# A row-wise softmax over 4096 rows: one tile's load shared between SyncE and GpSimd, and the first tile's load in one piece

## The chip, the cores and the metric

The kernel runs on one core of one Trainium2 chip. The metric is the device time of one execution in microseconds; the median of several runs is compared. Nothing is computed on the host.

## The reference

```python
batch, seq, vocab = 16, 256, 32768          # logits, fp32; temperature = 1.0
scaled = logits / temperature
scaled = scaled - scaled.max(axis=-1, keepdims=True)
exp_scaled = np.exp(scaled)
return (exp_scaled / exp_scaled.sum(axis=-1, keepdims=True)).astype(np.float32)
```

That is 4096 rows of 32768 numbers: 537 MB are read and 537 MB written.

## The kernel before

**Tiles.** Each row is cut into two halves of `_W` = 16384 numbers, and each half lies on one of the 128 partitions. A tile is 64 rows, that is 128 partitions of 64 KB each, 8 MB in all; there are 64 tiles. The buffer `xs` has three slots of 64 KB per partition, so tile g uses slot g mod 3, and it is worked on in place: load, exponentiate, scale, store.

**Work on a tile.** A tile is cut into three pieces of columns (six in the last two tiles). VectorE takes each piece's maximum (line 207); ScalarE exponentiates the piece with that maximum and sums it (line 267). Then VectorE brings the two halves of each row together in a few instructions of less than half a microsecond (lines 225 to 252), and the pieces are multiplied by their factors: the first on ScalarE (line 286), the others on VectorE (line 258). VectorE and ScalarE go through the tiles in order; the first four and the last three are written out, those between run in a loop.

**Transfers.** All DMAs are issued by SyncE (SP) in an order written out by hand: loads 0, 1, 2, store 0, load 3, store 1, store 2, and then load i and store i-1 in turn. A load of tile g waits until the store of tile g-3 has landed, because it overwrites its slot; a store waits until its tile is scaled (the wait stands at lines 150 to 155, the store at line 160, the load at line 143). SP issues in order, so a wait of one holds up all that stand behind it. A transfer is spread over the core's 16 DMA engines; its semaphore has risen by 16 when all of it has landed. Signals of one key add up over the transfers that share it.

**The places that the change touches.** `load_parts` says in which parts a tile is loaded. The first tile (g = 0) has two: 15360 columns of all rows, and the last `_NARROW` = 1024 columns. That second part is issued as 19 transfers (line 141) over the rows that `narrow_rows` gives:

```python
step = p // _FEW                       # 128 // 7 = 18
return [slice(q, step * _FEW, step) for q in range(step)] + [slice(step * _FEW, p)]
```

that is, 18 transfers of seven rows that are 18 apart, and one of the last two rows. The third tile (g = 2) is one transfer of 128 rows. In `landed`, VectorE waits for a part's semaphore before the first piece that touches it. Tile 3 uses the same slot and the same semaphores as tile 0, so its values there count on from tile 0's. GpSimd issues nothing in this kernel apart from four small constants.

Of the kernel before, what the change touches and what calls it, by code (L numbers as in the profile page):

```python
# [8 lines left out]
_W = 16384  # L9
# [1 line left out]
_PLAIN = ((6304, 5376, 4704), (0,))  # L11
_LATE = ((4096, 3072, 3072, 2048, 2048, 2048), (3, 4, 5))
_LAST_STORES = ((0, 4096), (4096, 6144), (10240, 6144))
_NARROW = 1024
_FEW = 7
_HEAD = 4
_TAIL = 3

# [45 lines left out]


def load_parts(g):
    if g == 0:
        return [(0, _W - _NARROW), (_W - _NARROW, _NARROW)]
    if g == 3:
        return [(0, _W // 2), (_W // 2, _W // 2)]  # L70
    return [(0, _W)]


def store_parts(g, n):
    if g == 0:
        return [(0, _W // 2), (_W // 2, _W // 2)]
    return list(_LAST_STORES) if g == n - 1 else [(0, _W)]


def narrow_rows(p):  # L80
    step = p // _FEW
    return [slice(q, step * _FEW, step) for q in range(step)] + [slice(step * _FEW, p)]


def order(n):
# [7 lines left out]
def kernel(  # L93
# [6 lines left out]
    nc = tc.nc  # L100
    inv_t = 1.0 / float(temperature)
    P = nc.NUM_PARTITIONS
    fp32 = mybir.dt.float32
# [7 lines left out]
    x = xf.rearrange("n (h v) -> (n h) v", h=2)  # L111
# [8 lines left out]
    X = nc.alloc_sbuf_tensor("xs", [P, _BUFS * _W], fp32)  # L120
    T = [nc.alloc_sbuf_tensor(f"t{q}", [P, 4 * most], fp32) for q in range(_BUFS)]
    E = [nc.alloc_sbuf_tensor(f"ee{q}", [P, 2 * most], fp32) for q in range(_BUFS)]
    J = [nc.alloc_sbuf_tensor(f"junk{q}", [P, 2 * most], fp32) for q in range(_BUFS)]
    R = [nc.alloc_sbuf_tensor(f"row{q}", [P, 4], fp32) for q in range(_BUFS)]
    sig = Signals(nc)
    stored = {}

    def load(g):
        p = Place(g, G)
        rows = slice(g * P, (g + 1) * P)  # L130
        for j, (s, n) in enumerate(load_parts(g)):
            if g >= _BUFS:
                parts = store_parts(g - _BUFS, G)
                for i, (a, m) in enumerate(parts):
                    if a < s + n and s < a + m:
                        nc.sync.wait_ge(*stored[g - _BUFS][i])
            where = slice(p.slot * _W + s, p.slot * _W + s + n)
            key = ("ld", j, *p.key)
            if g == 0 and j == 1:
                for some in narrow_rows(P):  # L140
                    sig.dma(key, nc.sync.dma_start(out=X[some, where], in_=x[some, s : s + n]))
            else:
                sig.dma(key, nc.sync.dma_start(out=X[:, where], in_=x[rows, s : s + n]))

    def store(g):
        p = Place(g, G)
        rows = slice(g * P, (g + 1) * P)
        stored[g] = []
        for i, (s, n) in enumerate(store_parts(g, G)):
            if p.looped:  # L150
                nc.sync.wait_ge(sig[("scaled", *p.key)], 2 * p.n)
            else:
                for group in (p.own, p.on_act):
                    for k in [k for k in group if k in p.over(s, n)][-1:]:
                        nc.sync.wait_ge(sig[("scaled", k, *p.key)], p.n)
            where = slice(p.slot * _W + s, p.slot * _W + s + n)
            stored[g].append(
                sig.dma(
                    ("st", i, p.slot),
                    nc.sync.dma_start(out=o[rows, s : s + n], in_=X[:, where]),  # L160
                )
            )

    class Work:

        def __init__(self, p):
            self.p = p
            q = p.slot
            K = self.K = len(p.pieces)
            self.t, self.e, self.j, self.r = T[q], E[q], J[q], R[q]  # L170
            self.tv = self.t[:, 0 : 4 * K].rearrange("p (a b k) -> p a b k", a=2, b=2)
# [18 lines left out]
        def landed(self, engine, k, seen):  # L190
            s, n = self.p.pieces[k]
            for j, (a, m) in enumerate(load_parts(self.p.g)):
                if a < s + n and s < a + m and j not in seen:
                    seen.add(j)
                    times = len(narrow_rows(P)) if self.p.g == 0 and j == 1 else 1
                    value = self.p.n16
                    if self.p.g == 3 and j == 1:
                        value, times = 16 * len(narrow_rows(P)) + 16, 1
                    engine.wait_ge(sig[("ld", j, *self.p.key)], value * times)

        def vector(self):
            t, e, r, tv, f, K = self.t, self.e, self.r, self.tv, self.j, self.K
# [85 lines left out]
    for what, g in order(G):  # L288
        if what == "L":
            load(g)  # L290
        else:
            store(g)
    for key in [key for key in sig.made if key[0] == "st"]:
        nc.sync.wait_ge(sig[key], sig.made[key])

    for engine, part in ((nc.vector, Work.vector), (nc.scalar, Work.scalar)):
# [43 lines left out]
```

## Time and profile before

| | us |
|---|---|
| median of 3 runs | 2486.93 (2486.84 to 2486.94) |
| the profiled execution | 2486.8 |
| its span | 2485.0 |
| VectorE busy | 1526.2 (61%) |
| ScalarE busy | 1325.7 (53%) |
| GpSimd busy | 0.2 |
| mean rate of the DMA engines | 432 GB/s |

The span runs from the first to the last instruction of the profiled execution; 1.8 us of its time lie around it. A line of the profile's timeline gives the start, the duration, the engine ("SPq" is SyncE issuing a DMA), the line of the kernel, the operation, output and input, how many instructions it sums up, and in square brackets how long the engine was idle before and what released it. Beside these views the trace holds a record of each DMA packet (start, duration, bytes; not which of the 16 engines moved it) and the time of each increment of a semaphore by a DMA engine. An engine's packets follow each other without a gap, so that its chain can be followed from packet to packet.

### The profile page before, as it was taken

What the parts mean: (1) busy time and instruction counts of PE and PEld (TensorE: products, weight loads), DVE (VectorE), ACT (ScalarE), POOL (GpSimd) and SP (SyncE); (2) the same over time, 40 slices, a digit from 0 to 9 for tenths busy, and PEclk for the clock granted to TensorE, in tenths of its full rate; (3) what the DMA queues carried; (4) which work ended last, traced back from release to release, by engine and by line L of the source; (5) the groups of instructions that cost most, each with busy time, mean ns of one, the idle gap of its engine ahead of it and who ended that gap; (6) DMA issues with size and microseconds to landing.
All of it is one profiled execution on the core that took longest, in us unless ns stands there. A gap on an engine that the chain in (4) does not pass through costs nothing.

```text
span 2485.0 us, 1689 instructions
## 1 busy us (share of the span) xinstructions
DVE 1526.2 (61%) x776; ACT 1325.7 (53%) x529; POOL 0.2 (0%) x4
## 2 busy tenths in 40 slices
DVE  5845665666656656566565665656656566566665
ACT  4744645546546455464554645546455464554654
POOL 0000000000000000000000000000000000000000
DMA  9999999999999999999999999999999999999998
GB/s 399 438 439 432 429 438 437 430 434 437 437 427 437 437 434 429 438 438 429 434 437 436 428 437 438 433 430 438 437 428 436 437 435 428 438 437 434 430 438 381
DMA packets 19267, 1073.78 MB, mean 432 GB/s; under 512 B 2240, under 2 KB 2240, under 8 KB 2368
## 3 DMA queue, kind: packets, MB, share of 16 engines
q1 hardware_dynamic: 19264, 1073.75, 99.8%
q14 instruction: 3, 0.02, 0.0%
HBM read 536.87 MB, written 536.87 MB: 432 GB/s over the span
## 4 chain that ended last, share of the span: by engine, by line
DMA 61%; DVE 28%; ACT 7%; issue 2%; SPq 0%; DVEq 0%
DMA xs<-in_logits_dram 59%; DVE t L207 21%; ACT xs L267 6%; DVE xs L258 6%; DMA out_dram<-xs 3%; SPq L160 0%; ACT ee L278 0%; DVE junk L252 0%; DVE t L225 0%; DVE row L249 0%; ACT xs L286 0%; DVE row L229 0%; DVE junk L236 0%; DVEq L299 0%; DVEq L223 0%
## 5 line engine op out<-in xcount | busy, mean ns | idle before, releaser
L267 ACT ACTIVATE xs<-xs,t 128x6304 f32<-128x6304 f32 (+5 forms) x198 | 932.1, 4707 | 1053.6 <-DVE t L207 1046.8
L207 DVE TENSOR_REDUCE t<-xs 128x1 f32<-128x6304 f32 (+5 forms) x198 | 1110.0, 5663 | 618.5 <-DMA xs<-in_logits_dram 618.5
L286 ACT ACTIVATE xs<-xs,junk 128x6304 f32<-128x6304 f32 (+1 forms) x68 | 355.6, 5236 | 45.0 <-DVE junk L252 45.0
L258 DVE TENSOR_SCALAR xs<-xs,junk 128x5376 f32<-128x5376 f32 (+2 forms) x130 | 358.8, 2803 | 2.3
L225 DVE LOAD_MASK_SELECT t<-t x64 | 0.9, 14 | 282.9 <-ACT xs L267 282.9
L278 ACT ACTIVATE ee<-t,row 128x6 f32<-128x6 f32 (+1 forms) x64 | 19.2, 300 | 35.3 <-DVE row L229 35.3
L267 ACT ACTIVATION_READ_ACCUMULATOR xs<-xs,t 128x1 f32 x198 | 37.0, 187 | 0.0
L236 DVE CUSTOM_DVE_ANT_1 junk<-ee,t 128x6 f32<-128x6 f32 (+1 forms) x64 | 10.7, 167 | 23.5 <-ACT ee L278 23.5
L252 DVE TENSOR_SCALAR junk<-ee,row 128x3 f32<-128x3 f32 (+1 forms) x64 | 14.6, 229 | 2.2
L249 DVE RECIPROCAL row<-row 128x1 f32<-128x1 f32 x64 | 10.5, 164 | 2.2
L229 DVE TENSOR_REDUCE row<-t 128x1 f32<-128x6 f32 (+1 forms) x64 | 10.2, 159 | 2.2
L225 DVE STREAM_SHUFFLE t<-t 128x6 f32<-128x6 f32 (+1 forms) x64 | 10.4, 163 | 0.5
L236 DVE DVE_READ_ACCUMULATOR2_ANT row<- 128x1 f32 x64 | 5.3, 83 | 0.0
L267 ACT ACT_TABLE_LOAD x1 | 1.3, 1283 | 0.9 <-SPq L119 0.9
L321 POOL MEMSET const-bfloat16-1.0<- 128x1 bf16 x1 | 0.1, 102 | 0.0
L321 POOL MEMSET const-uint8-127<- 128x1 uint8 x1 | 0.1, 102 | 0.0
L321 POOL MEMSET const-float32-0.0<- 128x1 f32 x1 | 0.1, 99 | 0.2 <-issue 0.2
L321 POOL MEMSET const-float32-1.0<- 128x1 f32 x1 | 0.1, 99 | 0.0
## 6 DMA issues: line engine op xcount, KB each, us to landing
out_dram<-xs SPq DMA_DIRECT2D x2, 4096.0 KB, 29.2
xs<-in_logits_dram SPq DMA_DIRECT2D x2, 4096.0 KB, 19.3
xs<-in_logits_dram SPq DMA_DIRECT2D x1, 7680.0 KB, 21.1
out_dram<-xs SPq DMA_DIRECT2D x2, 3072.0 KB, 19.5
out_dram<-xs SPq DMA_DIRECT2D x1, 2048.0 KB, 12.2
xs<-in_logits_dram SPq DMA_DIRECT2D x62, 48.1
out_dram<-xs SPq DMA_DIRECT2D x62, 29.1
xs<-in_logits_dram SPq DMA_DIRECT2D x18, 28.0 KB
```

The source lines that it names most:

```text
L207: m = v.tensor_reduce(out=t[:, k : k + 1], in_=self.piece(k), axis=mybir.AxisListType.X, op=A.max, negate=True,)
L225: v.stream_shuffle(out=t[:, 2 * K : 4 * K], in_=t[:, 0 : 2 * K], mask=swap), "sh"
L229: v.tensor_reduce(out=r[:, 0:1], in_=tv[:, :, 0, :], axis=mybir.AxisListType.XY, op=A.min),
L236: v.tensor_tensor_reduce(out=f[:, 0 : 2 * K].rearrange("p (a k) -> p a k", a=2), in0=self.ev, in1=tv[:, :, 1, :], scale=1.0, scalar=0.0, o ...
L249: self.done(v.reciprocal(out=r[:, 2:3], in_=r[:, 1:2]), "rc")
L252: v.tensor_scalar_mul(out=f[:, 0:K], in0=e[:, 0:K], scalar1=r[:, 2:3]), "f"
L258: v.tensor_scalar_mul(out=xs, in0=xs, scalar1=f[:, k : k + 1]), k, self.p.own
L267: s = a.activation(out=xs, in_=xs, func=Exp, bias=t[:, k : k + 1], scale=inv_t, accum_out=t[:, K + k : K + k + 1],)
L278: a.activation(out=self.ev, in_=self.tv[:, :, 0, :], func=Exp, bias=r[:, 0:1], scale=-1.0),
L286: self.scaled(a.mul(out=xs, in_=xs, mul=f[:, k : k + 1]), k, self.p.on_act)
L321: nc = _bacc.Bacc("TRN2", target_bir_lowering=False, num_devices=1)
```

## The change

The narrow loads of the first tile are gone: tile 0 is one transfer of 128 rows. The third tile's load has two parts now, with a semaphore each. SP issues the first: one transfer of the first half of the columns for all 128 rows, and then seven of the second half of the columns, each of 16 rows that are eight apart (rows r, r+8, r+16 ... for r = 0 to 6). The rows left over, 7, 15, ... 127, are loaded by GpSimd, which first waits until all eight of SP's transfers have landed. It issues four pairs: an "empty" transfer of 64-byte pieces into a spare buffer, and one of the data, with eight rows and two pieces of 8 KB per row. Both have the same shape but for the length of the pieces. VectorE waits for 128 (eight transfers) on the first semaphore and 64 (four) on the second before it starts on the third tile. At the end SP also waits for the empty transfers.

```diff
-_NARROW = 1024
-_FEW = 7
+_SPLIT = 2
 def load_parts(g):
-    if g == 0:
-        return [(0, _W - _NARROW), (_W - _NARROW, _NARROW)]
+    if g == _SPLIT:
+        return [(0, _W), (0, _W)]
...
-            if g == 0 and j == 1:
-                for some in narrow_rows(P):
-                    sig.dma(key, nc.sync.dma_start(out=X[some, where], in_=x[some, s : s + n]))
+            if g == _SPLIT and j == 0:
+                half = _W // 2
+                b = p.slot * _W
+                parts = [(slice(0, P), 0)] + [(slice(r, P, 8), half) for r in range(7)]
+                for some, c in parts:
+                    sig.dma(
+                        key,
+                        nc.sync.dma_start(
+                            out=X[some, b + c : b + c + half], in_=x[rows, c : c + half][some]
+                        ),
+                    )
+            elif g == _SPLIT:
+                nc.gpsimd.wait_ge(sig[("ld", 0, *p.key)], sig.made[("ld", 0, *p.key)])
+                for q in range(4):
+                    some = slice(7 + 64 * (q % 2), 64 + 64 * (q % 2), 8)
+                    c = _W // 2 + _W // 8 * (q // 2)
+                    here = X[some, p.slot * _W : (p.slot + 1) * _W].rearrange(
+                        "p (a f) -> p a f", f=_W // 4
+                    )
+                    there = x[rows][some].rearrange("p (a f) -> p a f", f=_W // 4)
+                    f = slice(_W // 8 * (q // 2), _W // 8 * (q // 2) + _W // 8)
+                    nothing = D[some, 32 * q : 32 * q + 32].rearrange("p (a f) -> p a f", a=2)
+                    sig.dma(
+                        ("spare",),
+                        nc.gpsimd.dma_start(out=nothing, in_=there[:, 2:4, 0:16]),
+                    )
+                    sig.dma(
+                        key, nc.gpsimd.dma_start(out=here[:, 2:4, f], in_=there[:, 2:4, f])
+                    )
...
-                    times = len(narrow_rows(P)) if self.p.g == 0 and j == 1 else 1
-                    value = self.p.n16
-                    if self.p.g == 3 and j == 1:
-                        value, times = 16 * len(narrow_rows(P)) + 16, 1
-                    engine.wait_ge(sig[("ld", j, *self.p.key)], value * times)
+                    value = 16 if j == 1 else self.p.n16
+                    value = [128, 64][j] if self.p.g == _SPLIT else value
+                    engine.wait_ge(sig[("ld", j, *self.p.key)], value)
```

More of the change, by code (lines that the diff above doesn't have):

```diff
@@ L77, in store_parts @@
     return list(_LAST_STORES) if g == n - 1 else [(0, _W)]
-def narrow_rows(p):
-    step = p // _FEW
-    return [slice(q, step * _FEW, step) for q in range(step)] + [slice(step * _FEW, p)]
 def order(n):
@@ L124 @@
     R = [nc.alloc_sbuf_tensor(f"row{q}", [P, 4], fp32) for q in range(_BUFS)]
+    D = nc.alloc_sbuf_tensor("spare", [P, 128], fp32)
     sig = Signals(nc)
@@ L292 @@
             store(g)
-    for key in [key for key in sig.made if key[0] == "st"]:
+    for key in [key for key in sig.made if key[0] in ("st", "spare")]:
         nc.sync.wait_ge(sig[key], sig.made[key])
```

## Prediction

> **What bounds the kernel now.** I read the page first, then the timeline, then the DMA share by windows, and last the records under them: each DMA packet's start, duration and bytes, and the arrival of each engine's completion signal.
>
> ```profile
> span 2485.0 us, 1689 instructions
> ...
> q1 hardware_dynamic: 19264, 1073.75, 99.8%
> ```
>
> The 16 DMA engines are busy for 99.8% of the span. No compute engine comes near that (VectorE 61%). The timeline, near the end of the loop, shows why the chain of waits nevertheless runs through compute:
>
> ```profile
> 2319.11 0.33 SPq L160 DMA_DIRECT2D out_dram<-xs  x1
> 2319.48 0.43 SPq L143 DMA_DIRECT2D xs<-in_logits_dram  x1
> 2328.90 17.34 DVE L207 TENSOR_REDUCE t<-xs 128x1 f32<-128x6304 f32 x3 [9.82 <-DMA xs<-in_logits_dram]
> ```
>
> The next store and load are queued at 2319, while the load before them lands only at 2328.9. The queue is never empty, so this is a race of 16 engines through fixed bytes, and the last one ends it. The last stores show that they do not arrive together (columns: window, its length, busy VectorE, ScalarE and GpSimd, clock, DMA share, GB/s):
>
> ```profile
> 2477.60:2480.10 2.50, 0.00 (x0) 0.00 (x0) 0.00 (x0) 1.00 0.41 177
> 2480.10:2481.40 1.30, 0.00 (x0) 0.00 (x0) 0.00 (x0) 1.00 0.09 38
> 2481.40:2483.40 2.00, 0.00 (x0) 0.00 (x0) 0.00 (x0) 1.00 0.06 25
> ```
>
> 0.41 of 16 is six to seven engines, 0.06 is one. By the packet records nine engines end at 2477.5 to 2477.8, seven at 2479.9, 2480.0, 2480.1, 2480.3, 2480.9, 2481.3 and 2483.3. The last of them I call the laggard. Where the gap comes from is seen at the start:
>
> ```profile
> 1.41 13.83 SPq L141 DMA_DIRECT2D xs<-in_logits_dram  x19
> 15.28 0.82 SPq L143 DMA_DIRECT2D xs<-in_logits_dram  x2
> 22.09 17.34 DVE L207 TENSOR_REDUCE t<-xs 128x1 f32<-128x6304 f32 x3 [22.09 <-DMA xs<-in_logits_dram]
> ...
> 50.84 0.82 SPq L160 DMA_DIRECT2D out_dram<-xs  x2
> 75.41 10.00 SPq L143 DMA_DIRECT2D xs<-in_logits_dram  x2
> 85.52 22.89 SPq L160 DMA_DIRECT2D out_dram<-xs  x2
> ```
>
> The 18 narrow transfers have seven rows each and ran on seven engines; the signals of the second tile's load come from nine engines within 0.65 us and from the other seven 2.9 to 3.3 us later. That gap stays to the end, and the laggard adds some 3 us more over the run (its offset is 3.3 at 160 us, 4.2 at 197 us after an 8 KB instruction fetch at 188 us, 6.2 at 2419 us).
>
> **Removing the narrow loads.** A 61440-byte packet takes 2.267 us, a 64 KB one 2.418 (2.414 from start to start). Eight rows of the first tile made whole cost each engine 8 x 0.151 = 1.2 us. Loads of the first tile end at about 21.1 on every engine; so the second tile would end at 21.1 + 1.2 + 8 x 2.414 = 41.6. In the trace it ends at 42.6 to 43.2 on the nine and 45.4 to 45.9 on the seven: gains of 1.3 us and 4.2 us. This is more than the bytes explain. Narrow packets take 0.159 us at first, but 0.25 to 0.34 (about 0.29) from 21.6 us on, once the nine engines have begun the second tile, and those engines' first 64 KB packets take 3.9 to 4.3 us. Transfers whose rows are dealt out unlike the 128-row ones crowd all 16 engines, by 0.29 / 0.159 = 1.8 or 4.1 / 2.418 = 1.7. That row matters again below.
>
> What else moves here costs nothing. SP drops 13.8 us of issues, ahead of which 21 us of packets lie queued. VectorE's first reduction starts 1.2 us later (23.3), and the first stores 1.2 us after 50.8; they queue behind the third tile's load, which runs to 62 us or later, so there are 10 us of cover.
>
> **The third tile, SP's part.** Each engine had eight packets of 64 KB: 8 x 2.414 + 0.02 = 19.33 us (0.02 is what a completion costs: 38.66 us per tile between early engines' signals, less 16 x 2.414, over two). Now it has eight packets of 32 KB and seven more of single rows: 15 x 1.209 + 8 x 0.02 = 18.3 us, so 1.0 us less, if the row-wise ones run freely. SP's eight issues (0.4 to 0.9 us each by L141's and L143's rows) start at about 2 us and are done long before 41 us.
>
> The seven row-wise transfers, each of 16 rows eight apart, hold 7 x 1.209 = 8.46 us of every engine. The trace has none like them. Bounds: a factor of 1.0 (narrow packets while alone) gives 0; 1.82 (narrow packets in the crowd) gives +6.9 us. I take 6.9: here, too, all 16 engines move rows that are not the ones they get in a 128-row transfer. [...]
>
> **GpSimd's part.** It waits for SP's eight transfers (count 128), then issues its eight; behind that wait stands nothing else on its queue. The data transfers carry 64 KB to each of eight engines in eight pieces of 8 KB: 8 x 0.309 (an 8 KB fetch of the instruction queue) = 2.5 us, and nothing to the other eight. The empty ones are 64-byte pieces (packets of up to 24 bytes take 7 ns): 0; the eight completions 0.2 us. If crowded by 1.82, the data cost 2.0 us more; I take that, since they are narrow rows again, and 0 as the other end. Which eight engines get them no row decides. Either transfers of eight rows always start at the same engine, as SP's of seven rows did, and the data falls on the late seven and one more; or they are dealt out in turn, and then each empty one uses up eight engines and the data always falls on the other eight, the early ones. I take the second, and price the first below. [...]
>
> Cover: VectorE waits for both counts, but takes up the third tile at 79.3 us only (80.5 now), when the part should have landed: SP's part ends at 41.6 + 18.3 + 6.9 = 67 us and eight issues at 1 to 2 us each, an estimate from SP's 0.4 to 0.9, follow. If it lands later, the third store, issued at 108, still has until the second store drains at 120.5: some 10 us more of cover.
>
> **Sum, in packet ends (2483.3 before).** Laggard: -4.2 - 1.0 + 0.2 + 6.9 = +1.9, so 2485.2. Data engines, the latest from 2477.8: -1.3, +1.6 (18.3 + 2.5 + 0.2 for 19.33, rounded), +6.9, +2.0: 2487.0. They are late now, by 3.7 us over 2483.3. The profiled execution took 2486.8 us (span 2485.0 and 1.8 around it; the median of the runs is 2486.93): **2490.5 us**, +0.15%. A difference under 0.2% (5.0 us) is about what a measurement of this kernel cannot tell from none, so bounds lie at 2482.0 and 2491.9.
>
> **Rivals.**
> 1. *No crowding.* Take out 6.9 and 2.0: laggard 2478.3, data engines 2478.1; the end moves by -5.0: 2481.8, or up to 2483.8 if only GpSimd's pieces crowd. For it: lone narrow packets ran at full rate, and packets of 32 KB in whole-tile shape (1.213 us) never crowd. Against it: the 4.1 us packets at 21 us. Chance 0.22, about half of it beyond 0.2%.
> 2. [...] With it goes GpSimd's data landing on the seven late engines instead: laggard -4.2 + 1.6 + 6.9 + 2.0 = +6.3, 2493.1. Together 0.25.
> 3. *GpSimd's part lands after 90 us*, beyond all cover: each further us costs one. Nothing in the trace asks for 20 us of issue: 0.03, slower.
> 4. My forecast, crowding at 1.5 to 1.9: 2488 to 2491.5: 0.50.
>
> **Numbers.** Faster is half of rival 1, 0.10; slower is rivals 2 and 3, 0.28; within 0.2% the rest, 0.62. The range runs from rival 1's end, 2481.6, to 2492.8, past rival 2's time; the forecast's own range is 2488 to 2491.5.
>
> **What would show it.** In the profile of the changed kernel: second tile landed on all engines by about 42 us (step 1); 32 KB packets of 1.2 us in the first half of the third tile and of about 2.2 us in the second (if 1.2: rival 1; if 2.4: rival 2); eight engines with 8 KB packets, of 0.3 or 0.55 us, and these among the nine early ones; VectorE's third tile starting near 80.5 us with no wait for DMA; at the end data engines last, the laggard 2 us ahead. The prediction is wrong if the row-wise packets run at 1.2 us, or if the end is set by a wait ahead of the third tile.

## The result, and the profile after

The changed kernel takes 2499.39 us (median of 5 runs, 2498.99 to 2500.15) against 2486.84 for the kernel before in the same job: a ratio of 1.0051, 95% interval 1.0039 to 1.0063. It is slower by 12.6 us, where 2490.5 was forecast and 2492.8 was the upper end. The profiled execution took 2499.1 us.

These lines of the page after the change answer to the two lines of before's page, with the new groups (line, engine, operation, tensors, count | busy, mean ns | idle before) and the new transfers (issuer, count, size, median us from issue to landing):

```profile
span 2497.3 us, 1690 instructions
...
q1 hardware_dynamic: 19232, 1073.23, 99.8%
q0 software_dynamic: 320, 0.53, 0.1%
...
L158 POOL DMA_DIRECT2D spare<-in_logits_dram x4 | 2.4, 590 | 69.4 <-DMA xs<-in_logits_dram 69.4
L161 POOL DMA_DIRECT2D xs<-in_logits_dram x4 | 2.2, 557 | 0.0
...
xs<-in_logits_dram SPq DMA_DIRECT2D x7, 512.0 KB, 58.0
...
xs<-in_logits_dram POOLq DMA_DIRECT2D x4, 128.0 KB, 17.3
```

The DMA engines are as busy as before, 99.8%, and the bytes are the same, so their packets must have become slower. GpSimd spends only 0.56 us on an issue, but its data land 17.3 us after it.

Where the time went can be read from the rate in 40 slices of some 62 us, first on the page of before and then on that of after:

```profile
GB/s 399 438 439 432 429 438 437 430 434 437 437 427 437 437 434 429 438 438 429 434 437 436 428 437 438 433 430 438 437 428 436 437 435 428 438 437 434 430 438 381
```

```profile
GB/s 378 403 420 428 436 429 434 427 435 434 431 436 431 435 437 429 436 437 431 435 437 431 432 437 431 435 435 436 430 437 431 436 432 434 435 432 435 431 437 396
```

The first four slices lack 21, 35, 19 and 4 GB/s: 79 / 435 x 62.3 = 11.3 us, nearly the whole difference. The changed transfers end in the second slice (100 us); the third starts at 125 us, when everything that was edited is over. So a part of the loss is a consequence and not a cost of the new transfers. The timeline of after, up to 150 us:

```profile
0.95 0.86 SPq L164 DMA_DIRECT2D xs<-in_logits_dram  x2
1.86 4.91 SPq L141 DMA_DIRECT2D xs<-in_logits_dram  x8
...
22.75 17.34 DVE L226 TENSOR_REDUCE t<-xs 128x1 f32<-128x6304 f32 x3 [22.75 <-DMA xs<-in_logits_dram]
...
69.86 0.69 POOL L158 DMA_DIRECT2D spare<-in_logits_dram  x1 [69.41 <-DMA xs<-in_logits_dram]
...
73.86 0.56 POOL L161 DMA_DIRECT2D xs<-in_logits_dram  x1
...
79.72 11.60 SPq L164 DMA_DIRECT2D xs<-in_logits_dram  x2
91.42 37.95 SPq L181 DMA_DIRECT2D out_dram<-xs  x2
...
100.29 17.34 DVE L226 TENSOR_REDUCE t<-xs 128x1 f32<-128x6304 f32 x3 [20.20 <-DMA xs<-in_logits_dram]
...
131.61 0.34 SPq L164 DMA_DIRECT2D xs<-in_logits_dram  x1
```

GpSimd has issued all by 74.4 us, yet VectorE waits 20.2 us and starts on the third tile at 100.29. SP therefore issues the third store only at 129 us (end of the 37.95 us at line 181; 108.4 before). The second store drains between 128.4 and 131.6 us by its signals, so nothing lies queued for the engines that finish first.

Later on the loop looks as before: at 2331 us a store and a load are queued 9.8 us before the load ahead of them lands.

```profile
2331.10 0.33 SPq L181 DMA_DIRECT2D out_dram<-xs  x1
2331.47 0.43 SPq L164 DMA_DIRECT2D xs<-in_logits_dram  x1
2340.86 12.38 DVE L226 TENSOR_REDUCE t<-xs 128x1 f32<-128x6304 f32 x2 [9.79 <-DMA xs<-in_logits_dram]
```

At the end (columns as in the windows of before) the engines come in within 3.6 us, by their signals from 2491.9 to 2495.5 us, where before nine came early, within 0.3 us:

```profile
2489.40:2491.90 2.50, 0.00 (x0) 0.00 (x0) 0.00 (x0) 1.00 0.96 413
2491.90:2493.40 1.50, 0.00 (x0) 0.00 (x0) 0.00 (x0) 1.00 0.49 213
2493.40:2495.50 2.10, 0.00 (x0) 0.00 (x0) 0.00 (x0) 1.00 0.11 47
```

**The account.** The packet records add up; they are those of the one profiled execution of each kernel. The mean over the 16 engines of the last signal is 2479.4 before and 2493.5 after, 14.1 us more; the last engine moves by 11.7 only, because before it stood 4.4 us behind the mean and now 2.0. All packets of a kind, divided by 16, give (us per engine, after less before):

| | predicted | measured |
|---|---|---|
| first tile whole, start | -2.6 | -2.6 |
| third tile, SP's 8 + 7 packets | +5.9 | +7.6 |
| GpSimd's pieces, with what they slow down | +2.35 | +3.1 |
| engines idle, 126 to 136 us | 0 | +0.8 |
| 64 KB packets slower than 2.418 us, past 130 us | 0 | +5.35 |
| sum | +5.7 | +14.2 (14.1 by the signals) |

The predicted column is the prediction's own terms, weighted by engines (nine at -1.3 and seven at -4.2 in the first row, eight of 16 at +4.7 in the third).

The row of the slow 64 KB packets is the largest miss. They are slow at the switches: counted at the transfer's end that lies nearest in time, of 5.6 us per engine 4.6 lie where a load ends and a store begins, and 1.0 where a store ends and a load begins. Before, the two are 0.2 and 0.05. I call what these packets lose past 130 us, at both switches, the switch loss: 5.6 us per engine here and 0.3 in before. It falls mostly on the last packet of the transfer that ends.

It starts with the third store, from 147 us on: the dry queue has brought the early half of the engines from 2.8 to 0.9 us ahead of the other, and now the last packet of each early engine takes 3.3 to 3.5 us, so that all 16 end the store within 0.4 us (8.7 engine-microseconds). Then the last packets of the next load take 2.9 to 4.0 us on all 16 (16.8 engine-microseconds, or 1.1 us per engine). It is not all early: half of the 5.6 us comes after 400 us, when the first and the last engine are 2 to 4 us apart again.

### The profile page after: what moved, and what is told of

Same layout as the page of the kernel before. It is cut to its first block, busy times and chain, and to the rows that moved or that the text cites. A ratio compares the mean times of both kernels' runs of the same rounds, so it can differ in the third digit from the quotient of the medians.

```text
span 2497.3 us, 1690 instructions
## 1 busy us (share of the span) xinstructions
DVE 1526.3 (61%) x776; ACT 1325.6 (53%) x529; POOL 4.8 (0%) x12
## 2 busy tenths in 40 slices
DMA packets 19555, 1073.78 MB, mean 430 GB/s; under 512 B 2480, under 2 KB 2480, under 8 KB 2480
## 3 DMA queue, kind: packets, MB, share of 16 engines
q1 hardware_dynamic: 19232, 1073.23, 99.8%
## 4 chain that ended last, share of the span: by engine, by line
DMA 62%; DVE 28%; ACT 7%; issue 2%; SPq 0%; DVEq 0%
DMA xs<-in_logits_dram 58%; DVE t L226 21%; ACT xs L286 6%; DVE xs L277 6%; DMA out_dram<-xs 3%; SPq L181 0%; ACT ee L297 0%; DVE junk L271 0%; DVE t L244 0%; DVE row L268 0%; ACT xs L305 0%; DVE row L248 0%; DVE junk L255 0%; DVEq L318 0%; DVEq L242 0%
## 5 line engine op out<-in xcount | busy, mean ns | idle before, releaser
L248 DVE TENSOR_REDUCE row<-t 128x1 f32<-128x6 f32 (+1 forms) x64 | 10.2, 159 | 2.2
## 6 DMA issues: line engine op xcount, KB each, us to landing
xs<-in_logits_dram POOLq DMA_DIRECT2D x4, 128.0 KB, 17.3
```

The source lines that it names most:

```text
L248: v.tensor_reduce(out=r[:, 0:1], in_=tv[:, :, 0, :], axis=mybir.AxisListType.XY, op=A.min),
```

## The experiments

Three things are asked: what the row-wise transfers cost (theory A: theirs is the whole loss), what GpSimd's late data cost (theory B: the queue that runs dry is the loss), and where the switch loss comes from. Theory C says that it comes from the order of the engines: when all 16 change from load to store at the same moment (they stand "abreast"), their packets slow down; when a group of them is some 3 us behind, it does not happen. The times of before in these jobs were 2486.74 to 2486.77 us. Repeated executions of some kernels differ by far more than those of before, so a range stands with each median.

**Only the narrow loads out** (the third tile whole):

```diff
-_SPLIT = 2
+_SPLIT = -1
```

> Only the narrow loads are taken out; the third tile is loaded whole, as before. Theory A (the loss of the change is the crowding of the row-wise transfers, 17.2 us for seven in the trace of after where 8.5 would be free; the narrow loads were a pure cost): the laggard gains 4.2 us, so about 2482.6 us. Theory C (the narrow loads had set seven engines 3 us behind the other nine, and engines that run abreast slow each other down for the rest of the run; after's 64 KB packets took some 4 to 5 us per engine more than 2.418 each, before's almost nothing past 60 us): 4.2 gained, 4 to 5 lost again, so 2486 to 2488, with 64 KB packets well over 2.418 us until 400 us or so.

Measured: 2486.55 us (2485.29 to 2503.59), ratio 1.0006 (0.9992 to 1.0021). The start was as forecast: the second tile landed at 41.5 to 42.1 us, the third at 62.0 to 62.5 (62.4 to 65.7 before). One execution of the ten took 2503.59, the others at most 2487.32. The engines are abreast, and the last packets of the third tile's load already lose 1.1 us per engine at 62 us, where the first store begins; the switch loss past 130 us is 3.8 us, in bouts at 159, 198, 237, 275, 314 us and later. So the step was right and its gain did not last. The timeline of this kernel shows no wait and no dry queue: VectorE takes up the third tile at 80.09 us and the third store is issued at 109.2, long before the next load's issue at 120.99.

```profile
80.09 17.33 DVE L226 TENSOR_REDUCE t<-xs 128x1 f32<-128x6304 f32 x3
82.81 26.36 SPq L181 DMA_DIRECT2D out_dram<-xs  x2
...
120.99 0.34 SPq L164 DMA_DIRECT2D xs<-in_logits_dram  x1
```

**All eight row groups by SP**, nothing by GpSimd:

```diff
-        return [(0, _W), (0, _W)]
+        return [(0, _W)]
...
-                parts = [(slice(0, P), 0)] + [(slice(r, P, 8), half) for r in range(7)]
+                parts = [(slice(0, P), 0)] + [(slice(r, P, 8), half) for r in range(8)]
...
-                    value = [128, 64][j] if self.p.g == _SPLIT else value
+                    value = 144 if self.p.g == _SPLIT else value
```

> The change without GpSimd: SP loads all eight groups of 16 rows that are eight apart. Theory A: the kernel without narrow loads plus 8 x (2.5 - 1.2) = 10 to 11 us, so 10 to 11 us over e1 whatever e1 is. Theory B (the loss of the change comes from the third tile's last rows landing at 100 us, so that the third store is issued at 129 only and the queue runs dry): the third tile lands at about 72 us here and VectorE does not wait for it, so nearly all the loss goes and this is within 3 us of e1.

Measured: 2495.65 us (2495.55 to 2497.81), ratio 1.0038 (1.0024 to 1.0052); 9.1 us more than the kernel without narrow loads. VectorE waits for nothing and the queue does not run dry. Row-wise packets of 32 KB take 2.54 us against 1.213 in the first half. Most of the loss is thus there without GpSimd: eight row-wise transfers cost 9.1 us, so seven cost some 8.0 (8.8 by their packets). The switch loss is 3.5 us per engine here, as in the kernel without narrow loads.

```profile
1.84 5.51 SPq L141 DMA_DIRECT2D xs<-in_logits_dram  x9
...
80.05 17.33 DVE L226 TENSOR_REDUCE t<-xs 128x1 f32<-128x6304 f32 x3
...
92.26 16.86 SPq L181 DMA_DIRECT2D out_dram<-xs  x2
```

**GpSimd's part without row-wise transfers.** SP loads the third tile as two halves of 128 rows; GpSimd loads its 16 half rows once more.

```diff
-                parts = [(slice(0, P), 0)] + [(slice(r, P, 8), half) for r in range(7)]
+                parts = [(slice(0, P), 0), (slice(0, P), half)]
...
-                    value = [128, 64][j] if self.p.g == _SPLIT else value
+                    value = [32, 64][j] if self.p.g == _SPLIT else value
```

> GpSimd's part without the row-wise transfers: SP loads all 128 rows of the third tile in two halves of the columns, and GpSimd, after that, loads its 16 half rows once more (the same data, 0.5 MB extra, 2.5 us on eight engines). Theory A: e1 plus 2.5 us at most on the engines with the data. Theory B: GpSimd's eight transfers again take some 26 us to land because each waits for its turn behind SP's packets; SP's part lands at about 61 instead of 69.5 us, so they land at about 90 instead of 100, VectorE starts the third tile there and the third store is issued at about 119, just as the second one drains: 0 to 3 us lost over e1 beyond the bytes. Theory C says nothing beyond e1, but a queue that runs dry sets all engines abreast again.

Measured: 2492.75 us (2491.17 to 2493.94), ratio 1.0024 (1.0014 to 1.0033). GpSimd's part alone costs 6.2 us over the kernel without narrow loads. It lands at 93.5 us; VectorE waits 13.36 us:

```profile
84.78 37.94 SPq L181 DMA_DIRECT2D out_dram<-xs  x2
...
93.64 17.34 DVE L226 TENSOR_REDUCE t<-xs 128x1 f32<-128x6304 f32 x3 [13.36 <-DMA xs<-in_logits_dram]
```

The third store goes out at 122.7 us, while the second drains at 122.1 to 124.9; after that all 16 engines end the third store within 0.4 us. By the packets the cost over the kernel without narrow loads is 1.5 us per engine for the 8 KB pieces, 1.3 for SP's 32 KB packets beside them, 0.7 idle, and 1.2 more switch loss: 4.7 in all, and by the mean of the last signals 4.8. SP's 32 KB packets also lose 1.0 us at 58 to 62 us, but GpSimd issues nothing before 62.9; that is the loss of 1.1 us that the kernel without narrow loads has there too. The second half of the columns, loaded over all rows, has no packet of the 2.54 us that the row-wise ones take.

**Without the four empty transfers:**

```diff
-                    sig.dma(
-                        ("spare",),
-                        nc.gpsimd.dma_start(out=nothing, in_=there[:, 2:4, 0:16]),
-                    )
```

> The change without the four empty transfers. Theory B: four transfers wait for their turns instead of eight, so the last rows land at about 85 instead of 100 us, the queue does not run dry, and 2 to 4 us of after's loss go: 2495.5 to 2497.5. Theory A and C: no more than 1 us from 2499.4. If GpSimd's transfers are dealt to the engines in turn, eight at a time, two fall on each half of the engines now, and the 2.9 us between two halves that after shows from 88 to 131 us are gone; if they always start at the same engine, the gap between the halves stays.

Measured: 2495.19 us (2494.17 to 2496.77), ratio 1.0033 (1.002 to 1.0045), 4.2 us less than the changed kernel by the medians and 2.3 by the profiled executions. The part lands at 89.6 us, and VectorE waits half as long:

```profile
89.71 17.34 DVE L222 TENSOR_REDUCE t<-xs 128x1 f32<-128x6304 f32 x3 [9.46 <-DMA xs<-in_logits_dram]
91.10 27.69 SPq L177 DMA_DIRECT2D out_dram<-xs  x2
```

So the empty ones move next to no data (0.013 us a packet), yet account for 10.6 us of the delay. In the changed kernel the signals show it: empty and data transfers end in turn at 76.6, 79.9, 82.0, 86.3, 88.7, 92.7, 95.1 and 100.2 us, an empty one 2.1 to 2.4 us after the transfer before it, one with data 3.3 to 5.1. Followed from packet to packet, the changed kernel's data fell as eight pieces on each of the same eight engines, and the empty ones on the other eight; without the empty ones the data transfers alternate between the two halves, and the gap of 2.8 to 3.3 us that the changed kernel has between the halves from 99 to 131 us is gone. The queue does not run dry, but the engines are abreast all the same (the last signal 1.2 to 1.4 us behind the first), and the switch loss is 5.4 us per engine. So the loss needs no dry queue.

**Half the narrow columns** in the kernel before:

```diff
-_NARROW = 1024
+_NARROW = 512
```

> Before's kernel with narrow loads of 512 columns instead of 1024: seven engines 1.4 us behind the nine instead of 2.9. What theory C has become from the trace of e1: engines that are abreast slow each other at the switch from a load to a store (3.6 us per engine over the run in e1, 5.1 in after, 0.1 in before); apart by more than a packet they do not. Theory C: the crowding at 21 us costs half as much, the laggard gains 2 us, and if 1.4 us apart are enough the time is about 2484.7; if not, some of the switches cost again: 2485 to 2488. Theory A (narrow loads are a pure cost; e1's trouble is something else that comes with a whole first load): half of e1's step at the start, no other change: between e1 and before, 2486.6 to 2486.8.

Measured: 2485.55 us (2485.23 to 2486.91), ratio 0.9996 (0.9986 to 1.0006). Seven engines stand 2.0 to 2.6 us behind, and the switch loss is 0.3 us. This was the lowest median of the study; its interval does not separate it from the kernel before.

**GpSimd earlier:** it waits for the first tile only.

```diff
-                nc.gpsimd.wait_ge(sig[("ld", 0, *p.key)], sig.made[("ld", 0, *p.key)])
+                nc.gpsimd.wait_ge(sig[("ld", 0, "h", 0)], 16)
```

> The change, but GpSimd waits for the first tile only, so its part lands by about 55 us and VectorE does not wait for it. Theory B: the queue does not run dry at 129 us; 3 to 4 us of after's loss go, as in e4. Theory C adds: the eight engines with GpSimd's data stay 2.9 us behind the others, since nothing sets them abreast again, so the switches cost nothing from then on and another 4 to 5 us go: 2490 to 2492. Without theory C 2495 to 2496. The crowding of the row-wise transfers stays in either case.

Measured: 2496.34 us (2495.91 to 2496.59), ratio 1.0038 (1.0024 to 1.0052). The part has landed before VectorE asks for it, the queue stays full, the two halves of the engines are 5 to 6 us apart for the whole run, and the switch loss is 0.2 us in place of 5.6.

```profile
23.29 0.69 POOL L158 DMA_DIRECT2D spare<-in_logits_dram  x1 [22.84 <-DMA xs<-in_logits_dram]
...
80.27 17.33 DVE L226 TENSOR_REDUCE t<-xs 128x1 f32<-128x6304 f32 x3
```

But the pieces now meet SP's loads: 64 KB packets before 60 us lose 1.2 us per engine more than in the changed kernel, the 32 KB ones 1.3 and the pieces themselves 0.4. Of 6.2 us that no longer arise (switch and idle), 2.9 are spent here, so the time missed what theory C forecast. By the time alone the run would fit the forecast without theory C (2495 to 2496); it is the packets that show the switch loss gone.

**Engines set apart on purpose.** The kernel without narrow loads, with spare loads by GpSimd after the first tile: 8 pairs of an empty transfer and one of 64 KB (the first kernel), the same without the empty ones (the second), or 4 pairs (the third). The spare data are used by nothing.

```diff
+    def spare_loads():
+        nc.gpsimd.wait_ge(sig[("ld", 0, "h", 0)], 16)
+        for q in range(8):
+            r = 64 + 32 * (q // 4) + q % 4
+            some = slice(r, r + 29, 4)
...
+            sig.dma(
+                ("spare",),
+                nc.gpsimd.dma_start(
+                    out=D[some, 0:2048].rearrange("p (a f) -> p a f", a=2),
+                    in_=x[some, 0:2048].rearrange("p (a f) -> p a f", a=2),
+                ),
+            )
...
```

> The kernel without narrow loads (e1, third tile loaded whole), and GpSimd loads 0.5 MB into a spare buffer, 64 KB on each of eight engines, with an empty transfer ahead of each so that it is always the same eight, and with rows four apart; the spare data are not used. Nobody waits for them. Theory C: these eight engines, which are not the laggards, are set 2.5 us behind, the switches cost nothing, and both groups end together: early engines 2477.6 - 1.3 + 2.7, laggard 2483.3 - 4.2, so about 2482.6 us, 4 us under both kernels. Theory A without C: e1 plus up to 2 us for the bytes: 2487 to 2489.

> e7 without the empty transfers: the same spare bytes, but dealt in turn to both halves of the engines, 32 KB on each engine, so that no group is set apart. Theory C: as e1 plus 1.3 us for the bytes, with packets over 2.418 us at the switches: 2486.5 to 2489. If instead it is the bytes or GpSimd's transfers that matter and not the distance between engines, e8 and e7 take the same time.

> e7 with half the spare bytes (32 KB on each of eight engines, four pairs of transfers instead of eight): the eight engines 1.2 us behind the others and half of e7's crowding at 25 to 60 us (about 1 us per engine). Theory C with the distance as the dose: less than a packet apart, so the switches cost as in e1, 2 to 3.6 us per engine, from early on and not only after 390 us as in e7: 2486 to 2488. If the distance plays no part, e7 less half its spare bytes and crowding: 2487.5 to 2488.5 as well, but with the loss of the switches starting as late as in e7; the place of the loss tells, not the sum.

Measured: 2489.6 us (2488.58 to 2490.53), ratio 1.0011 (1.0002 to 1.0021), with 8 pairs; 2490.03 (2489.35 to 2491.89), 1.0014 (1.0004 to 1.0023), without the empty ones; 2487.41 (2486.9 to 2489.22), 1.0004 (0.9995 to 1.0014), with 4 pairs. The first was expected near 2482.6 and missed. Its halves were 2.3 to 2.8 us apart and there was no switch loss until 372 us, but then it came, 2.8 us in all. The second was to be the control and is none: followed from packet to packet, all 64 of its pieces fell on the same eight engines, as in the first, and its halves were 2.6 us apart too (loss 2.4 us, from 469 us on). So data transfers of this shape were not dealt to the halves in turn, unlike those of the changed kernel; no run shows why. The third, with its engines some 1.5 us apart, lost from 140 us on, 1.9 us in all. So in these three the loss came later with engines 2.3 to 2.8 us apart (from 372 and 469 us) than with engines 1.5 us apart (from 140); the distance alone does not decide it.

**Other widths of the narrow columns** in the kernel before:

```diff
-_NARROW = 1024
+_NARROW = 256
```

> Before's kernel with narrow loads of 256 columns: seven engines set about 1 us behind. Theory C, with the distance as the dose (2.9 us in before and 2.0 to 2.6 in e5: no loss at the switches; 0 in e1: 3.6 us per engine): 1 us is less than a packet, so part of the switches cost again, 1 to 3 us per engine, and the time is 2485 to 2487. Theory A: the narrow loads' cost alone, on a line from e1 to before: 2486.6.

```diff
-_NARROW = 1024
+_NARROW = 2048
```

> Before's kernel with narrow loads of 2048 columns: seven engines set about 5.5 us behind. Theory C: no loss at the switches, as in before, but the crowding at 21 us costs twice as much: the laggard 4 us later than in before, 2490 to 2491.5. Theory A: the same on this side, so that the two differ only where the narrow loads shrink.

Measured: with 256 columns a median of 2500.86 us (2486.05 to 2511.32; about half the executions below 2494, half above 2507), ratio 1.0044 (1.0015 to 1.0073); with 2048 columns 2514.07 (2507.55 to 2520.91), ratio 1.0101 (1.0085 to 1.0118), expected at 2490 to 2491.5 and missed. With 2048 columns the late group starts 5.7 to 6.3 us behind and loses nothing until 354 us. By then it is 8.4 to 8.8 us behind, and from there on packets are slow at both switches, some 12 and 14 us per engine by the end, with some 1.9 us of idle engines between 400 and 2440 us that before has not. SP queues the next pair only 9.8 us before a load has landed on its last engine, so the early engines may then be out of work; that is my reading of the distance, not tested. In the profiled execution with 256 columns (2508.9 us) the late group begins 2.1 to 2.7 us behind, loses at the load's end from 159 us on all the same, is over 8 us behind from 622 us on, and goes the same way.

**One dry queue, and nothing else of the change.** The kernel before with a single wait added: VectorE starts the third tile only when the first half of the fourth has landed.

```diff
             seen = set()
+            if self.p.g == 2:
+                v.wait_ge(sig[("ld", 0, *Place(3, G).key)], Place(3, G).n16)
             for k in range(K):
```

> The kernel before with one more wait: VectorE starts the third tile only when the first half of the fourth has landed (91.5 to 94.7 us in before's trace, against its start at 79.3), so it starts near 94.7, the third store is issued near 123.4 and starts near 125.4 on all engines, while the second store drains at 120.5 to 123.8. The first tile's narrow loads stay, the third tile is loaded whole by SP, GpSimd does nothing. Direct cost: the seven late engines stand idle for about 1.6 us, the nine early ones for 4.9, so the last engine ends 1.6 us later at most: 2488.4. Theory C (engines set abreast lose time at the change from load to store): the excess of 64 KB packets past 130 us rises from 0.26 us per engine to 3.5 to 5.5, as in the runs without narrow loads, and the time is 2489 to 2493. Rival (those losses come with the first tile's whole load or with the split third tile, not with the engines' order): the excess stays under 0.5 us, and the time is 2485.5 to 2488.4.

Measured: 2497.0 us (2492.44 to 2511.02), ratio 1.0052 (1.0031 to 1.0073). The wait is one of 14.83 us, like the one that the change made:

```profile
75.26 9.98 SPq L143 DMA_DIRECT2D xs<-in_logits_dram  x2
85.35 38.33 SPq L160 DMA_DIRECT2D out_dram<-xs  x2
...
94.60 17.34 DVE L209 TENSOR_REDUCE t<-xs 128x1 f32<-128x6304 f32 x3 [14.83 <-DMA xs<-in_logits_dram]
```

The second store drains at 120.2 to 123.6 us with seven engines 3 us behind; the third starts on all 16 between 124.17 and 124.32. Up to its last packets, at 141 us, the packets are as before. With its end the switch loss is there: 13.3 engine-microseconds at 144 us, and 16.8 at 165 where the next load ends, as in the changed kernel (8.7 and 16.8). The engines stand idle 2.8 us more around 123 us; the late ones, which set the end, only some 1.1. So one wait that lets the engines start abreast is enough for the switch loss, with the first tile's narrow loads and the third tile's whole load in place.

In the whole profiled execution (2499.83 us; three of the eight took over 2506, four under 2494.5) packets past 130 us lose 9.9 us per engine (0.3 before), more than the 3.5 to 5.5 expected. Up to 2000 us it is 5.1. The other 4.8 come later, at both switches, when the last engine is some 8 us or more behind the first, as with 2048 and 256 narrow columns; the last slices of the rate show it.

```profile
GB/s 403 420 420 426 434 431 436 437 432 432 430 431 437 433 437 434 431 431 433 436 436 436 433 433 431 433 437 436 433 434 434 428 431 434 423 431 425 436 422 383
```

**Taken together.** Seven kernels had all engines within 1.5 us of each other when the third store ended (140 to 151 us): the changed one and those without narrow loads, with all rows by SP, with GpSimd's part alone, without empty transfers, with four spare pairs, and with the added wait. All seven lost at the switches from then on. In the other seven the last engine was 2.6 us or more behind the first; six of them, before's among them, lost next to nothing until 350 us, and the one with 256 columns lost from 159 us on.

## Why the prediction was wrong, step by step

- **Bound.** A race of 16 engines through fixed bytes: right, apart from the 0.8 us per engine at 126 to 136 us in which the queue was dry. The prediction took a packet's price as fixed once the start is over. That is the assumption behind its sum, and it failed.
- **Removing the narrow loads.** The step was right at its place: the second tile's packets ended at 41.1 to 41.7 us on all engines (41.6 forecast). The kernel with this edit alone kept none of the gain. The narrow loads cost the engines 2.6 us and spared them the switch loss (0.3 us against 3.8 past 130 us, and 1.1 more at 62 us).
- **SP's part.** The -1.0 held (first-half packets 1.213 us). The crowding term of 6.9 should have been 8.6: row-wise packets take 2.545 us in five of the seven transfers, 2.28 in one and 1.7 to 2.4 in the first, so the factor is up to 2.1 (2.0 in the mean) and not the 1.82 of the narrow packets. It is near the 2.4 us a packet by which the prediction would have known its rival 2; what makes it two no run shows.
- **GpSimd's part.** Until 88 us SP's queue was storing: there the 8 KB pieces took 0.309 us, as priced, and no 32 KB packet of the store beside them took more than 1.24 us (1.213 by itself). From 88.5 us on, with the fourth tile's load under way, 19 of the 64 pieces took 0.35 to 0.89 us, and SP's 32 KB packets lost 1.6 us per engine. The 2.0 us for crowding on eight engines, 1.0 in the mean of all, measured 1.8, and most of it fell on SP's packets, because the part landed so late. That the data falls on one half of the engines was right: the halves were 2.8 to 3.3 us apart from 99 us on, and without the empty ones they were not. That the transfers are dealt out in turn, on which the sum's data engines rest, was the author's choice and shown by no run then; these two traces agree with it, while the 64 pieces of the spare loads without empty transfers all fell on the same eight engines.
- **Cover.** This step failed most plainly. The eight issues were even cheaper than estimated (0.56 us instead of 1 to 2), but an issue is not a landing: beside SP's full queue each small transfer landed 2.1 to 5.1 us after the one before it, and the last rows landed at 100.2 us instead of about 80. This is rival 3, which had been given 0.03 since "nothing in the trace asks for 20 us of issue"; the time passed after the last issue (74.4 us) and not in it. Its price was wrong as well: landing 10.2 us beyond 90 did not cost 10.2 us. It left engines idle for 0.8 us, and cost more by what the prediction had no term for.
- **The missing term.** The late third store let the early engines run dry and brought them to within 0.9 us of the others; the switch loss that followed is 5.35 us per engine more than before. The kernel with one added wait shows that a wait of this kind alone makes such a loss, and the one with GpSimd earlier shows it gone (0.2 us) with the row-wise loads and GpSimd's part in place. The kernel without empty transfers never ran dry and lost as much (5.4 us per engine), with its last signal only 1.2 to 1.4 us behind the first.
- **Sum.** Of the some 8.5 us per engine between the predicted +5.7 and the measured +14.2, the switch loss is 5.35, the row-wise term 1.7, GpSimd's part 0.75 and the dry queue 0.8. Since the engines end more evenly than in before, the last engine moved by 11.7 us in the profiled execution. The range's upper end, 2492.8, was set past the time of rival 2, the one with 2.4 us a packet; no run had shown that factor of 2 then. The row-wise packets measured 2.0 in the mean, and the time lay 6.6 us beyond that end all the same.

What stays open: why packets slow down when the engines change from one transfer to the next together, and what starts a bout. The kernels with spare loads and those with other narrow widths show that neither the distance of the groups nor one moment decides it: 2.0 to 2.6 us apart was clean for 2480 us with 512 narrow columns, and 2.1 to 2.7 us was not with 256. So an early loss goes with engines that are close together, but the distance is no sure sign, and the added wait does not tell being abreast from having stood idle. Nor is it shown how the changed kernel would end if only its wait were taken away, since with GpSimd issued earlier the 64 KB packets before 60 us lose 1.2 us per engine more.

## What to carry to other kernels

Where all engines race through fixed bytes, price a change for the order in which the engines arrive too. Here a gap that looked like waste at the start (2.6 us per engine) went with a switch loss of 0.3 us, and the kernel without it lost 3.8; the queue that ran dry for a moment cost 0.8 us per engine itself, and 5.35 of switch loss came after it. Look for a transfer's landing and not for its issue alone: here eight small ones on a second queue, issued by 74.4 us beside a full queue, landed up to 100.2 us, and each empty one among them took 2.1 to 2.4 us of that. Before splitting a load by rows, compare the packets' duration with that of a load over all rows; here it doubled (2.545 us for 32 KB against 1.213).

## What was not expected of the hardware

- The switch loss: 64 KB packets of 2.418 us go up to 3.99 us where a transfer ends and the next begins, 5.6 us per engine over the changed kernel, and 0.3 before.
- Eight GpSimd transfers, issued in 4.6 us, took until 26 us after the last issue to land beside SP's queue; four of them were empty.
- GpSimd's 8 KB loads beside SP's stores slowed nothing (76.8 to 84.6 us in the changed kernel: 0.309 us each, the stores' 32 KB packets at most 1.24); beside SP's loads, SP's 32 KB packets went from 1.213 up to 2.3 us.
- In three kernels packets were slow at both switches once the last engine was some 8 us or more behind the first (8.4 to 8.8 us from 354 us on with 2048 narrow columns, over 8 from 622 us on with 256, after 2000 us with the added wait). The one with 2048 is the slowest kernel here, 2514 us.
- The same kernel with 256 narrow columns took 2486 us in some executions and 2511 in others.
